# Hybrid decoder step: operand tiles at one residue modulo 256 bytes, states in the scratch buffers' tails

## The chip, the cores and the metric

The kernel runs on one core of one Trainium2 chip. The metric is the device time of one execution in microseconds. Three runs of the kernel before took 1388.89, 1389.11 and 1389.2 us; the median is 1389.11.

## The reference

One layer of a hybrid decoder trunk, for 256 prompt tokens and 8 sample tokens (264 columns in all), model width 2048, all in float32:

```python
xn = rms_norm(x, g_mix)
z = xn @ w_in                      # 2048 x 3584: pool | lru x | lru gelu gate | conformer a | b
y_pool = pool_mixer(u_pool, pool_buf, ...) @ w_pool_br          # 512 -> 2048
xc, new_lru_buf = causal_dwconv(lru_buf, u_lru, w_lru_conv, b_lru_conv)      # 4 taps
h, h_last = rg_lru(xc, lru_h, ...)                              # 8 block-diagonal gates, scan
y_lru = (h * gelu(u_gel)) @ w_lru_br                            # 1024 -> 2048
vc, new_conf = causal_dwconv(conf_buf, c_a * sigmoid(c_b), w_conf_conv, b_conf_conv)  # 31 taps
y_conf = silu(layer_norm(vc, g_conf, b_conf)) @ w_conf_br       # 512 -> 2048
g_a, g_b, g_c = split(sigmoid(xn @ w_gate + b_gate), 3)
x = x + (g_a * y_pool + g_b * y_lru + g_c * y_conf) @ w_out
hid = square(relu(rms_norm(x, g_mlp) @ w_up))                   # 2048 -> 8192
x = x + hid @ w_down                                            # 8192 -> 2048
y = rms_norm(x, g_final)
```

The prompt starts from empty states; the sample tokens come with states of the pool (15 rows), the LRU's convolution (3 rows), its hidden vector, and the conformer's convolution (30 rows). All states are returned, brought forward by one step.

## The kernel before

*Products.* Features lie on the 128 partitions and the 264 tokens along the free dimension. Every matmul has 128 x 128 weights and 264 moving columns. To keep float32's precision, both sides are split into a high part, rounded to the `float32r` type, and a low part, the rest; `mm3` adds three matmuls: high weights by high operand (line 204), high weights by low operand (205), low weights by high operand (206). Line 913 issues the same three for the first four chunks in another order, so that operands can be used as they arrive.

*The stream of weights.* All weights come in chunks of 1,024 columns (two K tiles by four column tiles of 128), so a dense chunk is 24 matmuls: for each of its two K tiles, four column tiles by three. `weight_plan` lists the chunks in the order of use: `w_in`, then gates with the branch products of pool, LRU and conformer between them, `w_out`, and four times a quarter of `w_up` and the matching quarter of `w_down`. `dma_pair` (SP's queue, lines 148 and 156) loads two chunks into `raw`, which has 6 slots; `split` (lines 187 on ACT and 188 on DVE) makes `whi` and `wlo`, with 4 slots each, three chunks ahead of PE.

*Moving operands.* Tiles are allocated one after another, so their places follow from the sizes and the order.

- `A` holds 32 operand tiles, 16 high and 16 low: first `xn`, then the merged branches, then the hidden layer of quarters 0 and 2. It is addressed through `operand`: `SHIFT` = 56 floats further in, with a pitch of `PITCH` = 320 floats.
- `xn2` (four tiles that reuse the four scratch buffers `B`, in `bpart`) holds the second normalised input, in the same way: 8 operands in each.
- `L` and `LH` (one buffer, tag "L") hold the LRU's operands, and `Q` (tag "Q") those of the pool and the conformer. They are plain arrays `[P, 16, N]`, so their pitch is N = 264 floats, 1,056 bytes. In quarters 1 and 3 of the hidden layer `LH` holds the high parts and `Q` the low ones (`hid`).

*The rest.* DVE, ACT and POOL do normalisation, convolutions, gates and scans in between. Their order is written by hand: `stage` and `run_bg` deal pieces of it out, a chunk at a time, when the program is built; each engine then works strictly in that order and waits on semaphores.

*States.* All sample states lie in one tile `st`, of 2,036 floats a partition: 1,824 come in with one DMA (line 952) right after the first weights, in chunk 2; all go out with one DMA (line 983) in chunk 140. `pool_evac` (line 673) and `ca_evac` (line 582) add the newest row of the pool and conformer states; `diff` (709, 710) and the conformer's `products` (605) read them. `vext`, the conformer's padded input, lies at the end of the first 2,112 floats of the fourth scratch buffer; the first 2,112 floats of each are used as eight tiles of 264 (`B`), and the last 448 are in use for `xn2` alone.

*The end.* After the last product, DVE, ACT and POOL normalise `X` and write it to `y`, in two halves, and SP and ACT send it out (lines 1002 to 1026).

Of the kernel before, what the change touches and what calls it, by code (L numbers as in the profile page):

```python
# [9 lines left out]
F32 = mybir.dt.float32  # L10
F32R = mybir.dt.float32r
# [4 lines left out]
P = 128  # L16
# [22 lines left out]

S_POOL, S_LC, S_CC, S_H = 0, 512, 768, 1760  # L40
S_IN = 1824
# [3 lines left out]
PITCH = 320  # L45
SHIFT = 56
HEAD = N + 512
# [42 lines left out]
def hybrid_step(ctx: ExitStack, tc: tile.TileContext, first, par_in, st_in, wall, y_out, st_out):  # L90
# [11 lines left out]
    wlo = cpool.tile([P, NHI, CH], F32R, name="wlo")  # L102
    a_all = cpool.tile([P, SHIFT + 31 * PITCH + N], F32R, name="A")
    b_all = [cpool.tile([P, SHIFT + 7 * PITCH + N], F32, name=f"tmp{i}", tag=f"B{i}") for i in range(4)]
    qtmp = cpool.tile([P, 16 * N], F32, name="qtmp", tag="Q")
    X = cpool.tile([P, KD, N], F32, name="X")
    B = [b[:, :8 * N].rearrange("p (a n) -> p a n", a=8) for b in b_all]
    L = cpool.tile([P, 16, N], F32R, name="L", tag="L")
    G = cpool.tile([P, 24, N], F32, name="G")
    par = cpool.tile([P, NPAR], F32, name="par")  # L110
    st = cpool.tile([P, S_OUT], F32, name="st")
    rstd = cpool.tile([P, N], F32, name="rstd")
    ones = cpool.tile([P, P], F32, name="ones")
# [9 lines left out]
    def operand(t, k):  # L123
        at = SHIFT + k * PITCH
        return t[:, at:at + N]

# [99 lines left out]
    def later(n, fn):  # L226
        delayed.append((now[0] + n, fn))
# [56 lines left out]
    def rms_close(pk):  # L284
        ps = ones_mm(pk)
        inverse_root(rstd, ps[:, :N], 1.0, G[:, 9, :])
        spend(dve=1.4, act=0.8)
# [57 lines left out]
    def x_sum():  # L345
        nc.vector.tensor_tensor(sq4[:, 0:2, :], sq4[:, 0:2, :], sq4[:, 2:4, :], op=ALU.add)
        nc.vector.tensor_tensor(sq4[:, 0, :], sq4[:, 0, :], sq4[:, 1, :], op=ALU.add)
        spend(dve=1.2)
        later(1, lambda: total_fold(L[:, 0, :], G[:, 10, :], sq4[:, 0, :]))

    def x_rms():
        rms_close(L[:, 0, :])
        later(1, lru_x_scale)
# [24 lines left out]

    st_lc = st[:, S_LC:S_LC + 256].rearrange("p (c b k) -> p c b k", c=8, b=8)
    st_cc = st[:, S_CC:S_CC + 992].rearrange("p (c b k) -> p c b k", c=4, b=8)  # L380
    st_po = st[:, S_POOL:S_POOL + 512].rearrange("p (c b k) -> p c b k", c=4, b=8)
    st_h = st[:, S_H:S_H + 64].rearrange("p (c b) -> p c b", c=8)
    XC = G[:, 0:8, :]
# [6 lines left out]
    def LH(s):  # L390
        if not l_at:
            l_at.append(cpool.tile([P, 16, N], F32R, name="LH", tag="L"))
        return l_at[0][:, s, :]

    def two(c):
        return slice(2 * c, 2 * c + 2)
# [41 lines left out]
    def lru_conv_sample():  # L438
        tmp = CT.rearrange("p c n -> p (c n)")[:, :256].rearrange("p (c b k) -> p c b k", c=8, b=8)
        xs = XC[:, :, TP:N]  # L440

        def products():
            wb = pv("w_lru_conv").rearrange("p (c k) -> p c k", c=8)[:, :, None, :].to_broadcast([P, 8, 8, 4])
            nc.gpsimd.tensor_tensor(tmp, st_lc, wb, op=ALU.mult)
            nc.gpsimd.tensor_copy(st[:, O_LC:O_LC + 24].rearrange("p (c k) -> p c k", c=8), el[:, :, TP:TP + 3])

        def sums():
            nc.vector.tensor_reduce(xs, tmp, op=ALU.add, axis=AX.X)
            nc.vector.tensor_tensor(xs, xs, pv("b_lru_conv")[:, :, None].to_broadcast([P, 8, 8]), op=ALU.add)

        stage("lru", "pool", 1.0, [products])
        stage("lru", "dve", 0.5, [sums])
# [6 lines left out]

    def lo_two(t, at=8):  # L460
        return lambda c: t[:, at + 2 * c:at + 2 * c + 2, :]

    def hi_two(t):
        return lambda c: t[:, 2 * c:2 * c + 2, :]

    def lru_gate_mm(ct, c, j):
        assert "xc" in done
        hi, lo = whi[:, c % NHI, :], wlo[:, c % NHI, :]
        out = []
        for t in range(2):  # L470
            s = slice((2 * j + t) * P, (2 * j + t + 1) * P)
            ps = acc()
            mm3(ps, hi[:, s], lo[:, s], L[:, ct, :], L[:, 8 + ct, :], True, True)
            out.append(ps)
        nc.scalar.activation(RA[:, ct, :], out[0][:, :N], AF.Sigmoid, bias=pv("b_lru_a", ct))
        nc.scalar.activation(TM[:, ct, :], out[1][:, :N], AF.Sigmoid, bias=pv("b_lru_x", ct))
        spend(act=1.0)
        if ct % 2:
            def times():
                nc.vector.tensor_tensor(XC[:, ct - 1:ct + 1, :], XC[:, ct - 1:ct + 1, :], TM[:, ct - 1:ct + 1, :],  # L480
                                        op=ALU.mult)
                spend(dve=0.71)

            later(1, times)

    def lru_tail():
# [3 lines left out]
        def scratch():  # L490
            S.append(cpool.tile([P, 16, N], F32, name="lscr", tag="L")[:, 0:8, :])

# [30 lines left out]
        def sample():  # L523
            hs = H[:, :, TP:N]
            nc.gpsimd.tensor_tensor(TM[:, :, TP:N], TM[:, :, TP:N], st_h, op=ALU.mult)
            nc.gpsimd.tensor_tensor(hs, hs, TM[:, :, TP:N], op=ALU.add)
            nc.gpsimd.tensor_copy(st_h, hs)
            nc.gpsimd.tensor_copy(st[:, O_H:O_H + 8], H[:, :, TP - 1])

# [50 lines left out]
    def ca_evac(ct, ps):  # L580
        nc.vector.tensor_tensor(vext[:, ct, 30:], ps[:, :TP], SG[:, ct, :TP], op=ALU.mult)
        nc.vector.tensor_tensor(st_cc[:, ct, :, 30], ps[:, TP:N], SG[:, ct, TP:], op=ALU.mult)
        spend(dve=0.5)

    def conf():
# [17 lines left out]
        def products():  # L603
            wb = pv("w_conf_conv").rearrange("p (c k) -> p c k", c=4)[:, :, None, :].to_broadcast([P, 4, 8, 31])
            nc.gpsimd.tensor_tensor(tmp, st_cc, wb, op=ALU.mult)
            nc.gpsimd.tensor_copy(st[:, O_CC:O_CC + 120].rearrange("p (c k) -> p c k", c=4), vext[:, :, TP:TP + 30])

# [63 lines left out]
    def pool_evac(gi, ps):  # L671
        nc.vector.tensor_tensor(pext[:, gi, 15:], ps[:, :TP], rstd[:, :TP], op=ALU.mult)
        nc.vector.tensor_tensor(st_po[:, gi, :, 15], ps[:, TP:N], rstd[:, TP:], op=ALU.mult)
        spend(dve=0.5)
# [6 lines left out]
    def Q(s):  # L681
        if not q_at:
            q_at.append(cpool.tile([P, 16, N], F32R, name="Q", tag="Q"))
        return q_at[0][:, s, :]

    def pooling():
# [9 lines left out]
        def rows():  # L696
            nc.gpsimd.tensor_copy(st[:, O_POOL:O_POOL + 60].rearrange("p (c k) -> p c k", c=4),
                                  pext[:, :, TP:TP + 15])

        def diff(gi):  # L700
            w = 2 << gi
            s = part(gi + 1, gi)[:, 0, 15:]
            d = DU[:, gi, :]
            u = pext[:, gi, 15:]
            nc.vector.scalar_tensor_tensor(d[:, 16:TP], s[:, 16:], 1.0 / w, u[:, 16:], op0=ALU.mult, op1=ALU.subtract)
            nc.vector.scalar_tensor_tensor(s[:, :16], pv("count"), 1.0 / w, s[:, :16], op0=ALU.max, op1=ALU.mult)
            nc.vector.tensor_tensor(d[:, :16], s[:, :16], u[:, :16], op=ALU.subtract)
            us = st_po[:, gi, :, 15]
            nc.vector.tensor_reduce(d[:, TP:N], st_po[:, gi, :, 16 - w:], op=ALU.add, axis=AX.X)
            nc.vector.scalar_tensor_tensor(d[:, TP:N], d[:, TP:N], 1.0 / w, us, op0=ALU.mult, op1=ALU.subtract)  # L710
# [21 lines left out]
    def bpart(k):  # L732
        if not M:
            M.extend(cpool.tile([P, SHIFT + 7 * PITCH + N], F32R, name=f"xn2{i}", tag=f"B{i}") for i in range(4))
        return operand(M[k // 8], k % 8), operand(M[2 + k // 8], k % 8)
# [149 lines left out]
    def after(gi):  # L885

        name, _, _, m = groups[gi]
        if name == "w_in":
            if m == 2:
                lru_conv(range(4, 8))  # L890
                lru_conv_sample()
                mark("lru", "conv")
                stage_split("lru", 4, hi_two(L), lo_two(L), lambda c: XC[:, 2 * c:2 * c + 2, :])
                mark("lru", "xc")
# [41 lines left out]
    for i, ch in enumerate(chunks):  # L936
# [13 lines left out]
        if i == 2:  # L950
            nc.sync.dma_start(par, par_in)
            nc.sync.dma_start(st[:, :S_IN], st_in)
        kind, gi, c, _ = ch
# [26 lines left out]
        if i == len(chunks) - 4:  # L980
            nc.scalar.preload_act_table_set(ROOT)
        if i == 140:
            nc.sync.dma_start(st_out, st)
        if 5 <= i < 9:
# [15 lines left out]
    for h in range(2):  # L1000
        for k, t in enumerate((20, 21 + (KD - 2) % 3, 11)):
            nc.tensor.matmul(ps[h][:, :H2], ones, G[:, t, half[h]], start=k == 0, stop=k == 2)  # L1002
    out = [cpool.tile([P, SHIFT + 7 * PITCH + N], F32, name=f"y{h}", tag=f"B{h}")[:, :KD * H2]
           .rearrange("p (k n) -> p k n", k=KD) for h in range(2)]
# [131 lines left out]
```

## Time and profile before

| | us |
|---|---|
| median of 3 runs (lowest to highest) | 1389.11 (1388.89 to 1389.2) |
| span of the profiled execution | 1387.7 |
| PE busy, in that span | 1377.4 |
| DVE busy | 836.2 |
| ACT busy | 722.1 |
| POOL busy | 93.5 |

The profiled execution is one of its own; its span runs from the first to the last instruction on the chip, and the median of the runs stands 1.4 us above it. Memory is read at 184 GB/s over the span (252.57 MB).

How to read the rows: a group's row gives the line, the engine, the operation, what it writes and reads, the number of instructions, then the total busy time and the mean duration of one in ns, and the idle time before them with what ended it. PE is the matmul itself, PEld the load of its weights, which overlaps. A row by tile gives the shortest, median and longest duration in ns, and the first and last start in us. A row by window gives the window, its length, busy time and instructions of PE, the granted clock (1.00 is full speed), the mean busy share of the 16 DMA engines, and GB/s. A row of the timeline gives the start and the duration in us. A row of a wait gives who waited for whom: the sum in us, how often, the longest. A row of DMA issues ends with the KB of one and the us from issue to landing.

### The profile page before, as it was taken

How to read it: one execution, taken by the hardware profiler on the slowest of the kernel's cores; microseconds unless marked ns; L12 is line 12 of the kernel's file. 1: busy time of each engine (PE TensorE's matmuls, PEld its weight loads, DVE VectorE, ACT ScalarE, POOL GpSimd, SP SyncE). 2: the span in 40 equal slices, each digit the busy share in tenths (PEclk: the TensorE clock that was granted, in tenths of full speed). 3: DMA queues.
4: the chain of work that ended last, by engine and by line, in shares of the span. 5: the costliest groups of instructions: out<-in, count | busy, mean ns of one | idle time of the engine just before them, and what ended most of it. 6: DMA issues, size and time to landing. Idle time of an engine off the chain costs nothing.

```text
span 1387.7 us, 26639 instructions
## 1 busy us (share of the span) xinstructions
PE 1377.4 (99%) x11421; PEld 1375.6 (99%) x11421; DVE 836.2 (60%) x1052; ACT 722.1 (52%) x1021; POOL 93.5 (7%) x122
## 2 busy tenths in 40 slices
PE   9999999999999999999999999999999999999997
PEld 9999999999999999999999999999999999999997
DVE  8785887776766658566555445554455544455544
ACT  7757576666664645455544334543344533354544
POOL 0220010110102013010000000000000000000012
PEclk9999999999999999999999999999999999999999
DMA  9555555555565554655555555555555555555551
GB/s 355 180 178 189 189 187 195 182 182 184 181 214 181 182 185 156 209 178 173 198 184 185 183 183 186 183 182 178 178 184 183 184 186 182 187 183 184 179 177 72
DMA packets 39670, 257.49 MB, mean 186 GB/s; under 512 B 4352, under 2 KB 5504, under 8 KB 10624
## 3 DMA queue, kind: packets, MB, share of 16 engines
q1 hardware_dynamic: 39120, 255.19, 53.9%
q8 instruction: 89, 1.46, 0.4%
q10 hardware_dynamic: 432, 0.61, 0.1%
q14 instruction: 29, 0.24, 0.0%
HBM read 252.57 MB, written 3.21 MB: 184 GB/s over the span
## 4 chain that ended last, share of the span: by engine, by line
PE 99%; DVE 0%; DVEq 0%; ACT 0%; issue 0%
PE acc L204 33%; PE acc L205 33%; PE acc L206 32%; PE acc L913 1%; PE acc L298 0%; DVE y L1025 0%; DVE acc L1016 0%; DVEq L1115 0%; DVE G L1015 0%; DVE acc L1014 0%; PE acc L1002 0%; PE acc L281 0%; ACT rstd L1009 0%; DVE G L844 0%; DVE X L843 0%
## 5 line engine op out<-in xcount | busy, mean ns | idle before, releaser
L188 DVE TENSOR_TENSOR wlo<-raw,whi 128x1024 fp32r<-128x1024 f32 (+1 forms) x478 | 584.6, 1225 | 526.7 <-ACT whi L187 526.4
L187 ACT CAST whi<-raw 128x1024 fp32r<-128x1024 f32 (+1 forms) x478 | 495.3, 1039 | 599.5 <-PE acc L205 549.2
L204 PE MATMUL acc<-A,whi 128*128 128x264 f32 x1952 | 551.3, 282 | 0.0
L205 PE MATMUL acc<-A,whi 128*128 128x264 f32 x1952 | 551.2, 282 | 0.0
L206 PE MATMUL acc<-A,wlo 128*128 128x264 f32 x1952 | 548.6, 281 | 0.0
L206 PEld LDWEIGHTS acc<-A,wlo 128*128 128x128 f32 x1952 | 366.2, 188 | 0.0
L205 PEld LDWEIGHTS acc<-A,whi 128*128 128x128 f32 x1952 | 365.9, 187 | 0.0
L204 PEld LDWEIGHTS acc<-A,whi 128*128 128x128 f32 x1952 | 365.7, 187 | 0.0
L204 PE MATMUL acc<-xn,whi 128*128 128x264 f32 x1024 | 290.0, 283 | 0.0
L205 PE MATMUL acc<-xn,whi 128*128 128x264 f32 x1024 | 288.9, 282 | 0.0
L206 PE MATMUL acc<-xn,wlo 128*128 128x264 f32 x1024 | 287.2, 281 | 0.0
L206 PEld LDWEIGHTS acc<-xn,wlo 128*128 128x128 f32 x1024 | 192.2, 188 | 0.0
L205 PEld LDWEIGHTS acc<-xn,whi 128*128 128x128 f32 x1024 | 192.0, 188 | 0.0
L204 PEld LDWEIGHTS acc<-xn,whi 128*128 128x128 f32 x1024 | 191.7, 187 | 0.0
L205 PE MATMUL acc<-Q,whi 128*128 128x264 f32 x644 | 182.9, 284 | 0.0
L204 PE MATMUL acc<-LH,whi 128*128 128x264 f32 x640 | 182.3, 285 | 0.0
L206 PE MATMUL acc<-LH,wlo 128*128 128x264 f32 x640 | 181.9, 284 | 0.0
L205 PEld LDWEIGHTS acc<-Q,whi 128*128 128x128 f32 x644 | 121.7, 189 | 0.0
L206 PEld LDWEIGHTS acc<-LH,wlo 128*128 128x128 f32 x640 | 120.7, 189 | 0.0
L204 PEld LDWEIGHTS acc<-LH,whi 128*128 128x128 f32 x640 | 120.6, 188 | 0.0
L814 POOL TENSOR_TENSOR G<-G 128x264 f32<-128x264 f32 x28 | 25.7, 919 | 799.8 <-ACT G L812 798.9
L595 ACT ACTIVATE G<-tmp,par 128x256 f32<-128x256 f32 x120 | 54.3, 500 | 1.4 <-DVE G L609 0.7
(194 smaller groups left out, 792.7 us busy)
## 6 DMA issues: line engine op xcount, KB each, us to landing
raw<-wall_dram SPq DMA_DIRECT2D x226, 1024.0 KB, 4.9
raw<-wall_dram SPq DMA_DIRECT2D x12, 512.0 KB, 7.7
raw<-first_dram SPq DMA_DIRECT2D x6, 512.0 KB, 7.8
X<-first_dram SPq DMA_DIRECT2D x6, 264.0 KB, 7.3
raw<-wall_dram SPq DMA_DIRECT2D x5, 256.0 KB, 3.0
tmp<-first_dram SPq DMA_DIRECT2D x3, 388.0 KB, 4.8
so_dram<-st SPq DMA_DIRECT2D x1, 1018.0 KB, 9.4
st<-st_dram SPq DMA_DIRECT2D x1, 912.0 KB, 9.3
```

Of the source, the lines that this page charges most:

```text
L187: nc.scalar.copy(h[:, s], r[:, s])
L188: nc.vector.tensor_tensor(lo[:, s], r[:, s], f(h[:, s]), op=ALU.subtract)
L204: nc.tensor.matmul(ps[:, :N], whi_t, xh, start=first, stop=False)
L205: nc.tensor.matmul(ps[:, :N], whi_t, xl, start=False, stop=False)
L206: nc.tensor.matmul(ps[:, :N], wlo_t, xh, start=False, stop=last)
L595: nc.scalar.activation(dst[:, ct, :TP], vext[:, ct, k:k + TP], AF.Copy, scale=par[:, w:w + 1])
L814: nc.gpsimd.tensor_tensor(sq2, sq2, t, op=ALU.add)
L913: nc.tensor.matmul(pss[m][:, :N], w[:, i % NHI, s], x, start=i == kt == k == 0, stop=False)
```

## The change

`SHIFT` goes. `par` and `rstd` are allocated ahead of `A` instead of near the end, so that `A` and the tiles after it start at byte 96 modulo 256 by themselves. `L`, `LH` and `Q` get the pitch of 320 floats and are read through `operand` (one tile) and the new `operands` (several); splits and the LRU's square roots, which wrote two adjoining tiles of 264, now write two tiles 320 floats apart. `qtmp` and `L` thereby grow from 4,224 to 5,120 floats.

Room for that comes out of `st`, which shrinks to 532 floats: the pool and conformer states (376 floats a partition for each of the four groups) now lie in the four scratch buffers, from float 2,112 on (`tails`). They come in with four DMAs in chunks 13 to 16, after the weight pair that is issued in an even chunk, and go out with four in chunks 136 to 139. The conformer's `products` on POOL becomes four instructions, one for each group. On the host, the layout of the state arrays follows. The order of PE's instructions and what they wait for stay as they were.

```diff
-S_POOL, S_LC, S_CC, S_H = 0, 512, 768, 1760
+TAIL = 376
+S_SMALL = 4 * TAIL
+S_LC, S_H = S_SMALL, S_SMALL + 256
...
-SHIFT = 56
...
-    a_all = cpool.tile([P, SHIFT + 31 * PITCH + N], F32R, name="A")
-    b_all = [cpool.tile([P, SHIFT + 7 * PITCH + N], F32, name=f"tmp{i}", tag=f"B{i}") for i in range(4)]
-    qtmp = cpool.tile([P, 16 * N], F32, name="qtmp", tag="Q")
+    par = cpool.tile([P, NPAR], F32, name="par")
+    rstd = cpool.tile([P, N], F32, name="rstd")
+    a_all = cpool.tile([P, 32 * PITCH], F32R, name="A")
+    b_all = [cpool.tile([P, 8 * PITCH], F32, name=f"tmp{i}", tag=f"B{i}") for i in range(4)]
+    qtmp = cpool.tile([P, 16 * PITCH], F32, name="qtmp", tag="Q")
+    L = cpool.tile([P, 16 * PITCH], F32R, name="L", tag="L")
     X = cpool.tile([P, KD, N], F32, name="X")
...
-    L = cpool.tile([P, 16, N], F32R, name="L", tag="L")
     G = cpool.tile([P, 24, N], F32, name="G")
-    par = cpool.tile([P, NPAR], F32, name="par")
-    st = cpool.tile([P, S_OUT], F32, name="st")
-    rstd = cpool.tile([P, N], F32, name="rstd")
+    st = cpool.tile([P, S_OUT - S_SMALL], F32, name="st")
...
     def operand(t, k):
-        at = SHIFT + k * PITCH
-        return t[:, at:at + N]
+        return t[:, k * PITCH:k * PITCH + N]
+
+    def operands(t, k, n=2):
+        return t[:, k * PITCH:(k + n) * PITCH].rearrange("p (k c) -> p k c", k=n)[:, :, :N]
...
+    tails = [b[:, 8 * N:8 * N + TAIL] for b in b_all]
+    st_po = [t[:, :128].rearrange("p (b k) -> p b k", b=8) for t in tails]
+    st_cc = [t[:, 128:].rearrange("p (b k) -> p b k", b=8) for t in tails]
+
+    def state_move(i, move):
+        move(tails[i], slice(i * TAIL, (i + 1) * TAIL))
...
-            l_at.append(cpool.tile([P, 16, N], F32R, name="LH", tag="L"))
-        return l_at[0][:, s, :]
+            l_at.append(cpool.tile([P, 16 * PITCH], F32R, name="LH", tag="L"))
+        return operands(l_at[0], s.start) if isinstance(s, slice) else operand(l_at[0], s)
...
-            mm3(ps, hi[:, s], lo[:, s], L[:, ct, :], L[:, 8 + ct, :], True, True)
+            mm3(ps, hi[:, s], lo[:, s], operand(L, ct), operand(L, 8 + ct), True, True)
...
-            nc.gpsimd.tensor_tensor(tmp, st_cc, wb, op=ALU.mult)
+            for ct in g4:
+                nc.gpsimd.tensor_tensor(tmp[:, ct], st_cc[ct], wb[:, ct], op=ALU.mult)
...
-            q_at.append(cpool.tile([P, 16, N], F32R, name="Q", tag="Q"))
-        return q_at[0][:, s, :]
+            q_at.append(cpool.tile([P, 16 * PITCH], F32R, name="Q", tag="Q"))
+        return operands(q_at[0], s.start) if isinstance(s, slice) else operand(q_at[0], s)
...
         if i == 2:
             nc.sync.dma_start(par, par_in)
-            nc.sync.dma_start(st[:, :S_IN], st_in)
+            nc.sync.dma_start(small(S_SMALL, S_IN - S_SMALL), st_in[:, S_SMALL:])
+        if 13 <= i < 17:
+            state_move(i - 13, lambda t, s: nc.sync.dma_start(t, st_in[:, s]))
...
+        if 136 <= i < 140:
+            state_move(i - 136, lambda t, s: nc.sync.dma_start(st_out[:, s], t))
         if i == 140:
-            nc.sync.dma_start(st_out, st)
+            nc.sync.dma_start(st_out[:, S_SMALL:], st)
```

More of the change, by code (lines that the diff above doesn't have):

```diff
@@ L348, in x_sum @@
         spend(dve=1.2)
-        later(1, lambda: total_fold(L[:, 0, :], G[:, 10, :], sq4[:, 0, :]))
+        later(1, lambda: total_fold(operand(L, 0), G[:, 10, :], sq4[:, 0, :]))
     def x_rms():
-        rms_close(L[:, 0, :])
+        rms_close(operand(L, 0))
         later(1, lru_x_scale)
@@ L376, in softplus, with small @@
         eng.tensor_scalar(sp[:, 8:16], t2, -8.0, 0.0, op0=ALU.mult, op1=ALU.add)
[L379 to L382, printed above, removed]
+    def small(at, n):
+        return st[:, at - S_SMALL:at - S_SMALL + n]
+    tails = [b[:, 8 * N:8 * N + TAIL] for b in b_all]
+    st_lc = small(S_LC, 256).rearrange("p (c b k) -> p c b k", c=8, b=8)
+    st_po = [t[:, :128].rearrange("p (b k) -> p b k", b=8) for t in tails]
+    st_cc = [t[:, 128:].rearrange("p (b k) -> p b k", b=8) for t in tails]
+    st_h = small(S_H, 64).rearrange("p (c b) -> p c b", c=8)
+    def state_move(i, move):
+        move(tails[i], slice(i * TAIL, (i + 1) * TAIL))
     XC = G[:, 0:8, :]
@@ L444, in products @@
             nc.gpsimd.tensor_tensor(tmp, st_lc, wb, op=ALU.mult)
-            nc.gpsimd.tensor_copy(st[:, O_LC:O_LC + 24].rearrange("p (c k) -> p c k", c=8), el[:, :, TP:TP + 3])
+            nc.gpsimd.tensor_copy(small(O_LC, 24).rearrange("p (c k) -> p c k", c=8), el[:, :, TP:TP + 3])
         def sums():
@@ L458, in stage_split @@
                                for i in range(n)], gap)
[L460 to L464, printed above, removed]
     def lru_gate_mm(ct, c, j):
@@ L490, in scratch @@
         def scratch():
-            S.append(cpool.tile([P, 16, N], F32, name="lscr", tag="L")[:, 0:8, :])
+            S.append(operands(cpool.tile([P, 16 * PITCH], F32, name="lscr", tag="L"), 0, 8))
         def tanh(ct):
@@ L527, in sample @@
             nc.gpsimd.tensor_copy(st_h, hs)
-            nc.gpsimd.tensor_copy(st[:, O_H:O_H + 8], H[:, :, TP - 1])
+            nc.gpsimd.tensor_copy(small(O_H, 8), H[:, :, TP - 1])
         c4 = range(4)
@@ L581, in ca_evac @@
         nc.vector.tensor_tensor(vext[:, ct, 30:], ps[:, :TP], SG[:, ct, :TP], op=ALU.mult)
-        nc.vector.tensor_tensor(st_cc[:, ct, :, 30], ps[:, TP:N], SG[:, ct, TP:], op=ALU.mult)
+        nc.vector.tensor_tensor(st_cc[ct][:, :, 30], ps[:, TP:N], SG[:, ct, TP:], op=ALU.mult)
         spend(dve=0.5)
@@ L604, in products @@
             wb = pv("w_conf_conv").rearrange("p (c k) -> p c k", c=4)[:, :, None, :].to_broadcast([P, 4, 8, 31])
-            nc.gpsimd.tensor_tensor(tmp, st_cc, wb, op=ALU.mult)
-            nc.gpsimd.tensor_copy(st[:, O_CC:O_CC + 120].rearrange("p (c k) -> p c k", c=4), vext[:, :, TP:TP + 30])
+            for ct in g4:
+                nc.gpsimd.tensor_tensor(tmp[:, ct], st_cc[ct], wb[:, ct], op=ALU.mult)
+            nc.gpsimd.tensor_copy(small(O_CC, 120).rearrange("p (c k) -> p c k", c=4), vext[:, :, TP:TP + 30])
         def sums():
@@ L672, in pool_evac @@
         nc.vector.tensor_tensor(pext[:, gi, 15:], ps[:, :TP], rstd[:, :TP], op=ALU.mult)
-        nc.vector.tensor_tensor(st_po[:, gi, :, 15], ps[:, TP:N], rstd[:, TP:], op=ALU.mult)
+        nc.vector.tensor_tensor(st_po[gi][:, :, 15], ps[:, TP:N], rstd[:, TP:], op=ALU.mult)
         spend(dve=0.5)
@@ L696, in rows @@
         def rows():
-            nc.gpsimd.tensor_copy(st[:, O_POOL:O_POOL + 60].rearrange("p (c k) -> p c k", c=4),
+            nc.gpsimd.tensor_copy(small(O_POOL, 60).rearrange("p (c k) -> p c k", c=4),
                                   pext[:, :, TP:TP + 15])
@@ L707, in diff @@
             nc.vector.tensor_tensor(d[:, :16], s[:, :16], u[:, :16], op=ALU.subtract)
-            us = st_po[:, gi, :, 15]
-            nc.vector.tensor_reduce(d[:, TP:N], st_po[:, gi, :, 16 - w:], op=ALU.add, axis=AX.X)
+            us = st_po[gi][:, :, 15]
+            nc.vector.tensor_reduce(d[:, TP:N], st_po[gi][:, :, 16 - w:], op=ALU.add, axis=AX.X)
             nc.vector.scalar_tensor_tensor(d[:, TP:N], d[:, TP:N], 1.0 / w, us, op0=ALU.mult, op1=ALU.subtract)
@@ L733, in bpart @@
         if not M:
-            M.extend(cpool.tile([P, SHIFT + 7 * PITCH + N], F32R, name=f"xn2{i}", tag=f"B{i}") for i in range(4))
+            M.extend(cpool.tile([P, 8 * PITCH], F32R, name=f"xn2{i}", tag=f"B{i}") for i in range(4))
         return operand(M[k // 8], k % 8), operand(M[2 + k // 8], k % 8)
@@ L892, in after @@
                 mark("lru", "conv")
-                stage_split("lru", 4, hi_two(L), lo_two(L), lambda c: XC[:, 2 * c:2 * c + 2, :])
+                stage_split("lru", 4, lambda c: operands(L, 2 * c), lambda c: operands(L, 8 + 2 * c),
+                            lambda c: XC[:, two(c), :])
                 mark("lru", "xc")
@@ L1002, in hybrid_step @@
             nc.tensor.matmul(ps[h][:, :H2], ones, G[:, t, half[h]], start=k == 0, stop=k == 2)
-    out = [cpool.tile([P, SHIFT + 7 * PITCH + N], F32, name=f"y{h}", tag=f"B{h}")[:, :KD * H2]
+    out = [cpool.tile([P, 8 * PITCH], F32, name=f"y{h}", tag=f"B{h}")[:, :KD * H2]
            .rearrange("p (k n) -> p k n", k=KD) for h in range(2)]
@@ L1092 @@
     par = np.ascontiguousarray(np.concatenate(par, 1))
-    st = np.ascontiguousarray(np.concatenate([
-        _rows(a["state_pool"][0], 1), _rows(a["state_lru_conv"][0], 1), _rows(a["state_conf_conv"][0], 1),
-        _rows(a["state_lru_h"][0][:, None, :], 0)], 1))
+    big = np.concatenate([_rows(a["state_pool"][0], 1).reshape(P, 4, -1),
+                          _rows(a["state_conf_conv"][0], 1).reshape(P, 4, -1)], 2).reshape(P, -1)
+    st = np.ascontiguousarray(np.concatenate([big, _rows(a["state_lru_conv"][0], 1),
+                                              _rows(a["state_lru_h"][0][:, None, :], 0)], 1))
     wall = _stream({n: a[n][0] for n in ("w_in", "w_pool_grp", "w_pool_br", "w_lru_a", "w_lru_x", "w_lru_br",
@@ L1122, with rows_s @@
     ys = np.ascontiguousarray(y[TP:])[:, None]
-    def rows_s(at, c, k):
-        v = so[:, at:at + c * TS * k].reshape(P, c, TS, k)[..., 1:]
+    tails = so[:, :S_SMALL].reshape(P, 4, TAIL)
+    def rows_s(v, c, k):
+        v = v.reshape(P, c, TS, k)[..., 1:]
         return np.ascontiguousarray(v.transpose(2, 3, 1, 0).reshape(1, TS, k - 1, c * P))
@@ L1134 @@
     return (yp, ys, rows_p(O_POOL, 4, 15), rows_p(O_LC, 8, 3), h_p, rows_p(O_CC, 4, 30),
-            rows_s(S_POOL, 4, 16), rows_s(S_LC, 8, 4), h_s, rows_s(S_CC, 4, 31))
+            rows_s(tails[:, :, :128], 4, 16), rows_s(so[:, S_LC:S_LC + 256], 8, 4), h_s, rows_s(tails[:, :, 128:], 4, 31))
```

## The prediction

> **What bounds the kernel now.** I read the page first: which engine is busy, at what clock, and what the chain that ended last is made of.
>
> ```profile
> span 1387.7 us, 26639 instructions
> PE 1377.4 (99%) x11421; PEld 1375.6 (99%) x11421; DVE 836.2 (60%) x1052; ACT 722.1 (52%) x1021; POOL 93.5 (7%) x122
> PEclk9999999999999999999999999999999999999999
> PE 99%; DVE 0%; DVEq 0%; ACT 0%; issue 0%
> ```
>
> PE is busy for 1377.4 of 1387.7 us at the full granted clock, and the chain is PE for 99%. Next the waits, longest first, to see whether PE ever waits for an operand.
>
> ```profile
> ACT whi L187 <- PE acc L205: 549.2, 350, 3.7
> ...
> PE acc L298 <- PEq L1109: 0.8, 1, 0.8
> ```
>
> The casts of the streamed weights wait for PE to give their buffers back, 549.2 us in all; of PE there is only the 0.8 us at its start. So the time is the number of matmuls times their spacing, plus a head and a tail. The mean duration in the rows (about 282 ns) is not the spacing: matmuls overlap. For the spacing I took, by tile, the first and last start in two `w_down` quarters, first the one that reads `A`, then the one that reads `LH` and `Q`.
>
> ```profile
> L204 PE MATMUL acc<-A,whi x256: 285/285/285, 728.6 to 820.4; 128*128 128x264 f32 x128
> L206 PE MATMUL acc<-A,wlo x256: 279/279/279, 728.8 to 820.6; 128*128 128x264 f32 x128
> L204 PE MATMUL acc<-LH,whi x256: 278/285/294, 912.9 to 1006.0; 128*128 128x264 f32 x128
> L206 PE MATMUL acc<-LH,wlo x256: 278/283/297, 913.1 to 1006.3; 128*128 128x264 f32 x128
> ```
>
> Same 768 matmuls, same shapes: 728.6 to 820.6 against 912.9 to 1006.3, 92.0 against 93.4 us. The durations are also constant for `A` (285/285/285) and scattered for `LH` (278 to 297). To have it to 0.01 us, I cut the windows from the first matmul of a stage to the first after it: four times the branch products of pool and LRU together, those of the conformer, and three `w_down` quarters, the first of which is the `A` one. The counts include the two or three matmuls still running at the left edge.
>
> ```profile
> 243.16:260.63 17.47, 17.47 (x146) 1.00 0.55 183
> 283.67:301.16 17.49, 17.49 (x146) 1.00 0.53 183
> 347.24:364.73 17.49, 17.49 (x147) 1.00 0.53 183
> 410.81:428.29 17.48, 17.48 (x146) 1.00 0.62 213
> 520.72:544.14 23.42, 23.42 (x194) 1.00 0.44 149
> 728.58:820.74 92.16, 92.16 (x770) 1.00 0.54 184
> 912.90:1006.38 93.48, 93.48 (x770) 1.00 0.53 181
> 1282.86:1376.35 93.49, 93.49 (x771) 1.00 0.41 139
> ```
>
> The `A` quarter is 92.16 us for 768, **120.0 ns** each. The `LH`/`Q` ones are 93.48, **121.7 ns**, at the same clock and with no more DMA traffic (shares 0.53 and 0.41 against 0.54). What differs is where the moving operand lies. Tiles lie in the order of their allocation. In the built program `raw` starts at byte 1,152 of a partition and all tiles up to `G` are multiples of 256 bytes long, so each starts at byte 128 modulo 256. `A(k)` lies `SHIFT` (56 floats, 224 bytes) further in, at 96, and its pitch of 1,280 is 5 x 256: every `A` and `xn2` operand is at 96 modulo 256. `L`, `LH` and `Q` have a pitch of 1,056 = 4 x 256 + 32, so tile k starts at 128 + 32k modulo 256: only k = 7 and 15 lie at 96, k = 4 and 12 at 0.
>
> Does the time follow that within one tile? The timeline of the second column group of the `LH`/`Q` quarter has twelve matmuls in a row on each k; these are the first rows of k = 4, 5, 6, 7 and 8, residues 0, 32, 64, 96 and 128:
>
> ```profile
> 942.09 0.29 PE L204 MATMUL acc<-LH,whi 128*128 128x264 f32 x1
> ...
> 943.57 0.29 PE L204 MATMUL acc<-LH,whi 128*128 128x264 f32 x1
> ...
> 945.04 0.28 PE L204 MATMUL acc<-LH,whi 128*128 128x264 f32 x1
> ...
> 946.50 0.29 PE L204 MATMUL acc<-LH,whi 128*128 128x264 f32 x1
> ...
> 947.95 0.28 PE L204 MATMUL acc<-LH,whi 128*128 128x264 f32 x1
> ```
>
> Steps of 1.48, 1.47, 1.46 and 1.45 us: 123.3, 122.5, 121.7 and 120.8 ns a matmul. The run at 96 is the fastest of the four.
>
> **The change part by part.**
>
> *Operands.* `L`, `LH` and `Q` get the pitch of 1,280, and every operand tile starts at 96 modulo 256 (`par` and `rstd` now stand ahead of `A`: 58,496 + 1,200, up to the next 32, + 1,056 = 60,768 = 237 x 256 + 96). `A` and `xn2` move by exactly 2,048 bytes, so their 120.0 ns should stay. `LH` and `Q` come to lie 20,480 bytes apart, as `A`'s high and low halves do; weights, PSUM and PE's order are untouched. I take 120.0 ns for all. Branch products: 17.47 + 17.49 + 17.49 + 17.48 = 69.93 us for 4 x 144 matmuls, against 69.12 at 120.0: 0.81 us. Conformer: 23.42 against 192 x 0.120 = 23.04: 0.38. The two quarters: 93.48 and 93.49 against 92.16: 1.32 + 1.33. The LRU gate blocks and the pool groups have no windows of their own:
>
> ```profile
> L204 PE MATMUL acc<-L,whi 128*128 128x264 f32 x16 | 4.5, 283 | 0.0
> ```
>
> 16 of each of three products, and 4 x 3 for the pool groups, 60 matmuls at the mean excess of the others, 3.84 us / 2,304 = 1.67 ns: 0.10. Together **3.94 us**. The other end of the bound is the `LH` row at 96 itself, 120.8 ns; I take 120.0 because the 1.45 us includes the step from a neighbour at another residue, which the `A` rows, with no such neighbour, don't have.
>
> *States.* One 912 KB load becomes 160 KB at the old place and four pieces of 188 KB (1,504 bytes a partition) in SP's queue, after the weight pairs of chunks 20, 22 (two pieces) and 24. The rows that bound it:
>
> ```profile
> raw<-wall_dram SPq DMA_DIRECT2D x226, 1024.0 KB, 4.9
> ...
> st<-st_dram SPq DMA_DIRECT2D x1, 912.0 KB, 9.3
> ...
> y_dram<-y SPq DMA_DIRECT2D x2, 198.0 KB, 2.0
> ...
> par<-par_dram SPq DMA_DIRECT2D x1, 150.0 KB, 7.6
> 42.36 15.66 SPq L148 DMA_DIRECT2D raw<-wall_dram  x3
> L673 DVE TENSOR_TENSOR st<-acc,rstd x4: 161/164/164, 74.3 to 75.6; 128x8 f32<-128x8 f32 x4
> ```
>
> The three pairs are issued from 42.36 to 58.02. A piece lands in between 2.0 (198 KB, DMA otherwise quiet) and 9.3 us (the whole old load in the crowded head); I take 4.9, that of a weight pair beside the same stream. The last lands by 58.4 + 9.3 = 67.7 at the latest. The four `L673` results, which now go into the pieces and so wait for them, come from 74.3 on: 6.6 us of cover, value 0. Behind them on DVE stand the weight splits, and PE waits for those, so from there on a late piece would cost first their lead and then PE time. The weight loads queued behind the pieces have cover too: chunk 20's load is issued at 42.36 and cast here:
>
> ```profile
> 54.78 1.04 ACT L187 CAST whi<-raw 128x1024 fp32r<-128x1024 f32 x1
> 4.56 12.47 PE acc L913 x96
> ```
>
> PE ends its first four chunks at 17.03 and takes 24 x 0.120 = 2.88 us for each later one, so it needs chunk 20 at about 63.1. Less cast and subtraction, 1.04 and about 1.2, the load may land until 60.8, 18.4 us after issue; it takes 4.9, which leaves 13.5. The states' way out, five DMAs of the old 1,018 KB, goes out beside the gates from about 400 us on and nobody reads it: 0.
>
> *POOL and the splits.* The conformer products are four instructions instead of one.
>
> ```profile
> 173.86 3.13 POOL L605 TENSOR_TENSOR G<-st,par 128x992 f32<-128x992 f32 x1 [35.95 <-DVE st L582]
> 192.27 1.18 DVE L609 TENSOR_REDUCE G<-G 128x32 f32<-128x992 f32 x1
> L444 POOL TENSOR_TENSOR G<-st,par x1: 644/644/644, 83.0 to 83.0; 128x256 f32<-128x256 f32 x1
> L428 DVE TENSOR_TENSOR G<-G,tmp x6: 1218/1219/2548, 58.7 to 87.4; 128x1024 f32<-128x1024 f32 x6
> L339 DVE TENSOR_TENSOR G<-G x3: 1250/1253/1253, 29.2 to 33.8; 128x1056 f32<-128x1056 f32 x3
> ```
>
> Four like `L444` are 2.6 us, four times the whole row 12.5; the sum that needs them starts at 192.27, 15.3 us after `L605` ends, so even the upper end, 9.4 us more, is covered. Splits and roots that wrote 528 contiguous elements now write 2 x 264 with a gap: `L428`, in the code four pieces of 256, has 1.19 ns an element, `L339`, in one, 1.19 too. Cost 0.
>
> *Head and tail.* The first 96 matmuls (12.47 us) wait for loads that the change leaves alone. `X`, `G` and `y` start 32 bytes lower modulo 256:
>
> ```profile
> L849 DVE TENSOR_TENSOR X<-X,acc x63: 420/423/430, 751.0 to 1375.1; 128x264 f32<-128x264 f32 x63
> ```
>
> `L849` goes through all eight residues of `X` and spreads by 10 ns of 423, 2.4%; on the about 11.3 us of the tail that is at most 0.3 either way. I take 0.
>
> Sum: 1387.7 - 3.9 = 1383.8 us of span. The median of the runs, 1389.11, is 1.4 above that profile's span, so **1385.2 us**.
>
> **The rivals.** *Half the gain.* `LH` and `Q` settle at the 120.8 ns of their own rows at 96: 2,364 x (121.67 - 120.83) = 2.0 us, 1387.1. For it: these are their own rows. Against it: the jump between residues is in them.
>
> *No change: the residue is not the cause*, and the scatter belongs to these two tiles, whatever their place: 1389.1. The four steps from 1.48 to 1.45 inside one tile speak against it. [...]
>
> *Slower: the pieces hold up the weights.* If each of the three pieces ahead of chunk 24's load took the old load's 9.3 us and they went one after another, it would come 27.9 us later; 13.5 are covered, 14.4 fall on PE, less the 3.9 gained: 1399.6. It decides from 17.4 us of delay on. For it: 1,504-byte rows in the middle of the stream. Against it: the traffic there is 0.53 to 0.56 of the engines' time, 188 KB is less than a fifth of a weight pair, which lands in 4.9, and the 912 KB of before at the crowded head did no harm.
>
> **How the numbers follow.** Forecast 0.83, half the gain 0.07, no change 0.05, slower 0.05. The range, 1384.6 to 1386.6, is the forecast with 0.3 for head and tail and the 0.31 us between the lowest and highest run below, and above with 0.8 more, for a part of the matmuls staying over 120.0 ns. A change under 0.2% (2.8 us) can't be told from none, so half the gain counts as the same: faster 0.84, same 0.11, slower 0.05.
>
> **What would show it.** Right: the `LH`/`Q` quarters take 92.16 us and their durations are as constant as `A`'s, the first of them starts at about 911.6 (1.3 earlier) and the last matmul of the stream ends 3.9 earlier. Half: 92.8 us. Wrong on the cause: 93.5 us again. Wrong on the cover: a row of PE waiting for `wlo` between 45 and 80 us, or of DVE `L673`'s successor waiting for a state DMA.

## The result and the profile after

The changed kernel took 1385.35 us (median of 7 runs, 1384.94 to 1385.68); the kernel before, beside it, 1389.2 (7 runs, 1388.89 to 1390.07). The ratio is 0.9971, with a 95% interval of 0.9961 to 0.9982: 0.3% faster, small but clear of the spread of the runs. 1385.2 was predicted.

The page of the changed kernel, the lines on the span, the engines and the chain:

```profile
span 1383.8 us, 26656 instructions
PE 1373.5 (99%) x11421; PEld 1371.8 (99%) x11421; DVE 835.4 (60%) x1052; ACT 721.5 (52%) x1021; POOL 94.4 (7%) x125
PE 99%; DVE 0%; DVEq 0%; ACT 0%; issue 0%
```

The span is 3.9 us shorter and PE is busy for 3.9 us less with the same 11,421 matmuls; the rest of the page hardly moved. Where they went is seen in the view by windows, cut as before from the first matmul of a stage to the first after it: four times the branch products of pool and LRU, those of the conformer, the `A` quarter of `w_down`, and the two `LH`/`Q` quarters.

```profile
243.12:260.40 17.28, 17.28 (x146) 1.00 0.53 187
283.44:300.72 17.28, 17.28 (x146) 1.00 0.53 184
346.80:364.08 17.28, 17.28 (x146) 1.00 0.54 184
410.16:427.44 17.28, 17.28 (x146) 1.00 0.55 187
519.86:542.90 23.04, 23.04 (x194) 1.00 0.43 153
727.35:819.51 92.16, 92.16 (x770) 1.00 0.54 184
911.67:1003.83 92.16, 92.16 (x770) 1.00 0.54 183
1280.31:1372.47 92.16, 92.16 (x770) 1.00 0.41 141
```

Each of these stages now has 120.0 ns a matmul. The branch products gave 17.47 + 17.49 + 17.49 + 17.48 - 4 x 17.28 = 0.81 us, the conformer's 0.38, the quarters 1.32 and 1.33. From the first LRU gate block to the first of these windows, by the starts in the traces, it is 139.68 us in place of 139.78: 0.10 for the gate blocks and the pool groups. Together that is the 3.94 of the sum. The view by tile, for `LH` in the first of the two quarters, shows that the scatter of the durations (278 to 297 before) is gone too:

```profile
L207 PE MATMUL acc<-LH,whi x256: 282/283/283, 911.7 to 1003.5; 128*128 128x264 f32 x128
L209 PE MATMUL acc<-LH,wlo x256: 285/285/285, 911.9 to 1003.7; 128*128 128x264 f32 x128
```

The covers held. The first rows below are the state pieces (the view of line 961 and the time to landing of its DMAs), then the DVE instruction that needs them, then the POOL products and the sum behind them (timeline).

```profile
L961 SPq DMA_DIRECT2D tmp<-st_dram x4: 425/432/434, 42.8 to 58.1; - x4
...
DMA to landing us min/median/max: 4.9/5.2/5.9
...
L679 DVE TENSOR_TENSOR tmp<-acc,rstd x4: 164/166/167, 74.4 to 75.6; 128x8 f32<-128x8 f32 x4
...
172.62 4.03 POOL L611 TENSOR_TENSOR G<-tmp,par 128x248 f32<-128x248 f32 x4 [34.68 <-issue]
...
192.26 1.18 DVE L615 TENSOR_REDUCE G<-G 128x32 f32<-128x992 f32 x1
```

The last piece landed by 58.1 + 5.9 = 64.0, ten us before it is used, and the four products ended at 176.7, 15.6 before the sum. PE waited for no weights and no states: its only waits are 0.8 us at its start and 0.3 us for the last normalisation in the tail, both as before.

```profile
PE acc L301 <- PEq L1121: 0.8, 1, 0.8
...
PE acc L1013 <- DVE G L850: 0.3, 1, 0.3
```

### The profile page after: what moved, and what is told of

Read it like the earlier page. It is cut to its first block, busy times and chain, and to the rows that moved or that the text cites. A ratio compares the mean times of both kernels' runs of the same rounds, so it can differ in the third digit from the quotient of the medians.

```text
span 1383.8 us, 26656 instructions
## 1 busy us (share of the span) xinstructions
PE 1373.5 (99%) x11421; PEld 1371.8 (99%) x11421; DVE 835.4 (60%) x1052; ACT 721.5 (52%) x1021; POOL 94.4 (7%) x125
## 4 chain that ended last, share of the span: by engine, by line
PE 99%; DVE 0%; DVEq 0%; ACT 0%; issue 0%
PE acc L209 33%; PE acc L208 33%; PE acc L207 32%; PE acc L920 1%; PE acc L301 0%; DVE y L1036 0%; DVE acc L1027 0%; DVEq L1127 0%; DVE G L1026 0%; DVE acc L1025 0%; PE acc L1013 0%; PE acc L284 0%; ACT rstd L1020 0%; DVE G L850 0%; DVE X L849 0%
## 5 line engine op out<-in xcount | busy, mean ns | idle before, releaser
L209 PE MATMUL acc<-xn,wlo 128*128 128x264 f32 x1024 | 291.7, 285 | 0.0
```

Source lines behind the costliest of these rows:

```text
L209: nc.tensor.matmul(ps[:, :N], wlo_t, xh, start=False, stop=last)
```

## The experiments

Two questions stayed open. Was it the placement that gave the 3.9 us, or did the moved states and tiles give or take something beside it? And is it the operand's own place that sets the spacing, or the step between places, or the place relative to something else? Each edit is to the changed kernel. Residue means the start of an operand modulo 256 bytes; the weights start at 128 unless said otherwise. "Inner" spacings are means over the starts in the trace, with the first and the last of the twelve steps on one operand left out. e3 to e7 were run once each.

### e1: the old pitch back

`L`, `LH` and `Q` are read through functions of their own, `lq` for one tile and `lqs` for several. The first tile starts 8 floats further in, at residue 128 as before:

```diff
+    def lqs(t, k, n=2):
+        at = 8 + k * N
+        return t[:, at:at + n * N].rearrange("p (k c) -> p k c", k=n)[:, :, :N]
```

> The changed kernel, with L, LH and Q back at a pitch of 264 floats and at the residues they had before (128 + 32k modulo 256); the states stay in the tails and everything else as changed. Theory (the start of the moving operand modulo 256 sets the spacing; states, POOL and the strided splits cost nothing): the LH/Q quarters take 93.5 us again, the conformer's products 23.4, and the time is that of the kernel before, 1389.2. Rival (the moved states, the four POOL products or the new places of X and G gain or cost something that the operands hide): a time that differs from 1389.2 by that something, by more than 0.5 us, with A's quarter off 92.16.

Measured: 1389.05 us (10 runs), ratio to the kernel before 0.9998 (0.9989 to 1.0008). The windows for the conformer's products, the `A` quarter and the two others:

```profile
520.30:543.69 23.39, 23.39 (x194) 1.00 0.43 151
728.14:820.30 92.16, 92.16 (x770) 1.00 0.53 183
912.46:1005.94 93.48, 93.48 (x770) 1.00 0.53 182
1282.42:1375.90 93.48, 93.48 (x770) 1.00 0.40 139
```

With the residues of before, the stages take their old 23.4 and 93.48 us, states in the tails or not. So the placement of `L`, `LH` and `Q` is the whole gain, and the rest of the change costs nothing that can be measured: the kernel before had 1389.3 us beside this run, 0.25 more.

### e2: one pitch, another residue

`lq` and `lqs` again, with the changed kernel's pitch and 40 floats further in:

```diff
+    def lq(t, k):
+        return t[:, 40 + k * PITCH:40 + k * PITCH + N]
```

> The changed kernel with every L, LH and Q operand 160 bytes further in, so all of them start at residue 0 modulo 256, with the pitch of 1280 bytes kept. Theory (the residue itself sets the spacing): 123.6 ns a matmul as k = 4 and 12 had before, 94.9 us a quarter, 2,364 x 3.6 ns = 8.5 us more than the changed kernel: 1393.9. Rival (what cost was the step from one residue to another, or a pitch that is no multiple of 256): 120.0 ns, 92.16 us a quarter, 1385.4.

Measured: 1393.44 us (7 runs), ratio to the kernel before 1.0029 (1.0018 to 1.004). The conformer's products, the `A` quarter, the first `LH`/`Q` quarter:

```profile
521.40:545.06 23.66, 23.66 (x194) 1.00 0.43 148
729.52:821.68 92.16, 92.16 (x770) 1.00 0.54 184
913.84:1008.56 94.72, 94.72 (x770) 1.00 0.52 179
```

123.3 ns a matmul with a pitch of 1,280 bytes and no step between residues: the even pitch alone is worth nothing, and a badly chosen residue is 4.1 us worse than the uneven one of before. The rival falls. The place matters.

### e3: a scan of residues

```diff
+    def stepped(t, k, step, of):
+        at = k * PITCH + (step * (of % 16)) % 60
+        return t[:, at:at + N]
...
-        return operand(a_all, k)
+        return stepped(a_all, k, 4, k)
...
-        return operand(M[k // 8], k % 8), operand(M[2 + k // 8], k % 8)
+        return stepped(M[k // 8], k % 8, 1, k), stepped(M[2 + k // 8], k % 8, 1, k)
```

> The changed kernel with A(k) starting 16 bytes further in for each k, so its operands go through the residues 96, 112, ... to 240 and 0 to 64 modulo 256 (14 steps, then k = 15 at 96 again), and xn2 operand k starting 4 bytes further in for each k (96 to 156). L, LH and Q stay at 96. Theory: the spacing within a run of twelve matmuls on one k depends on the residue, as in LH and Q before: at 0 about 123.6 ns, 32 and 64 about 122, 128 and 160 about 121.4, 192 about 120.7, 224 about 122, at 96 120.0; what residues between multiples of 32 give is not known. The time then is some 1.5 ns x 5,952 matmuls of A = 9 us over the changed kernel, and some more for xn2. Rival (steps between residues): only the first matmul of a run is longer, by about 5 ns, the rest have 120.0; under 3 us more.

Measured: 1398.85 us (one run). Inner spacings of `A`: 122.3 ns at 0, 119.9 at 16, 120.6 at 48, 122.7 at 64, 120.1 at 96 and 144, 121.3 to 122.1 from 160 to 240. In steps of 4 bytes, `xn2` has 120.0 at 96 and 120, but 124.9 at 100 and 125.7 at 116. The first rows of neighbouring operands in one column group of `w_up` show it, at 96, 100 and 104, then at 116, 120 and 124:

```profile
663.84 0.28 PE L211 MATMUL acc<-xn,whi 128*128 128x264 f32 x1
...
665.28 0.28 PE L211 MATMUL acc<-xn,whi 128*128 128x264 f32 x1
...
666.77 0.29 PE L211 MATMUL acc<-xn,whi 128*128 128x264 f32 x1
...
671.18 0.28 PE L211 MATMUL acc<-xn,whi 128*128 128x264 f32 x1
...
672.69 0.29 PE L211 MATMUL acc<-xn,whi 128*128 128x264 f32 x1
...
674.13 0.28 PE L211 MATMUL acc<-xn,whi 128*128 128x264 f32 x1
```

Twelve matmuls took 1.44 us at 96 and 120, 1.49 at 100 and 1.51 at 116. So it isn't a matter of coarse alignment: 16, 48 or 144 serve as well as 96, or nearly, and 4 bytes can cost 5 ns.

### e4: the weights moved

```diff
+    par = cpool.tile([P, NPAR], F32, name="par")
+    rstd = cpool.tile([P, N], F32, name="rstd")
     whi = cpool.tile([P, NHI, CH], F32R, name="whi")
     wlo = cpool.tile([P, NHI, CH], F32R, name="wlo")
-    par = cpool.tile([P, NPAR], F32, name="par")
-    rstd = cpool.tile([P, N], F32, name="rstd")
```

> The changed kernel with par and rstd allocated ahead of whi and wlo instead of behind them: the weights start at residue 96 modulo 256 instead of 128, and all operands stay where they are. Theory (the moving operand's own place decides): 120.0 ns everywhere, 1385.4. Rival (the place relative to the weights decides, best when the operand lies 32 bytes below them modulo 256): an operand at the weights' own residue had 121.3 ns (128) before, so some 1.4 ns x 11,300 matmuls = 16 us more, about 1401.

Measured: 1387.76 us (one run), between the two expectations. Windows of 100 us, with every operand at 96, show why:

```profile
100.00:200.00 100.00, 100.00 (x836) 1.00 0.57 192
450.00:550.00 100.00, 100.00 (x826) 1.00 0.51 174
728.00:828.00 100.00, 100.00 (x835) 1.00 0.54 188
```

836 matmuls in 100 us are 120 ns each, 826 are 121.3 (the counts include two or three still running at the left edge). Matmuls of the same kind on the same places have two spacings, for hundreds of us at a time. Neither theory had that.

### e5: the scan with the weights moved

The edits of e3 and e4 together.

> The residue scan of e3 (A in steps of 16 bytes, xn2 in steps of 4) with the weights at residue 96 as in e4. Theory, place of the operand alone: the spacing by residue as in e3 (A: 16, 96 and 144 at 120, 0 at 122.3, 64 at 122.7, 224 at 122.1 ns). Rival, distance between operand and weights: the same profile 32 bytes lower, so 240, 64 and 112 at 120.0, and 224 (122.3), 32 (122.7) and 192 (122.1) the slow ones, 96 at 121.1 as 128 had.

Measured: 1399.99 us (one run). Inner spacings of `A` in ns:

| residue | e5 (weights at 96) | e3 at the same residue | e3 32 bytes higher |
|---|---|---|---|
| 240 | 119.96 | 121.70 | 119.93 |
| 64 | 119.99 | 122.66 | 120.12 |
| 112 | 120.01 | 121.33 | 120.09 |
| 16 | 120.53 | 119.93 | 120.61 |
| 32 | 122.78 | 121.76 | 122.66 |
| 224 | 122.80 | 122.13 | 122.28 |

The table has six of the fourteen residues that can be compared. Over all fourteen, e5 differs from e3 32 bytes higher by 0.17 ns in the mean, and from e3 at the same residue by 0.94. So the pattern moved with the weights, by their 32 bytes. In the timeline it is seen from the first rows of neighbouring operands in one column group: in e3 those at 240, 0, 16 and 32,

```profile
793.75 0.29 PE L211 MATMUL acc<-A,whi 128*128 128x264 f32 x1
...
795.21 0.29 PE L211 MATMUL acc<-A,whi 128*128 128x264 f32 x1
...
796.70 0.29 PE L211 MATMUL acc<-A,whi 128*128 128x264 f32 x1
...
798.14 0.28 PE L211 MATMUL acc<-A,whi 128*128 128x264 f32 x1
```

and in e5 those at 208, 224, 240 and 0:

```profile
792.10 0.29 PE L211 MATMUL acc<-A,whi 128*128 128x264 f32 x1
...
793.56 0.29 PE L211 MATMUL acc<-A,whi 128*128 128x264 f32 x1
...
795.04 0.29 PE L211 MATMUL acc<-A,whi 128*128 128x264 f32 x1
...
796.49 0.28 PE L211 MATMUL acc<-A,whi 128*128 128x264 f32 x1
```

Twelve matmuls at 0 took 1.49 us in e3, those at 224 took 1.48 in e5, and the next operand was quick again (1.44, 1.45). The theory that the operand's own residue decides falls here, and the distance to the weights takes its place. It does not fit everywhere: with steps of 4 bytes, e5's 100 has 125.9 ns where e3's 132 has 122.5, and over the eight residues that can be compared the mean difference is 0.8 ns, against 1.3 at the same residue. The two largest misses, at 96 and 100, are the first operands behind the jump back from 156; whether what ran before matters was not tested.

### e6: high and low parts apart

Only `Q` goes through e2's `lq` and `lqs`:

```diff
-        return operands(q_at[0], s.start) if isinstance(s, slice) else operand(q_at[0], s)
+        return lqs(q_at[0], s.start) if isinstance(s, slice) else lq(q_at[0], s)
```

> The changed kernel with Q alone at residue 0, L and LH at 96. In the two LH/Q quarters of w_down two matmuls of three then read at 96 and one at 0. Theory, each matmul pays for its own operand: 120.0 + 3.33 / 3 = 121.1 ns, 93.0 us a quarter; the products on Q alone (pool, conformer) at 123.3. Rival, the pair matters (a high and a low part at different residues): another value, 120.0 or over 122.

Measured: 1389.76 us (one run); the first `LH`/`Q` quarter:

```profile
912.41:1006.27 93.86, 93.86 (x771) 1.00 0.53 181
```

93.86 / 768 = 122.2 ns, where one third of e2's excess would give 121.1: one bad operand of three costs two thirds of what three cost. The theory falls and the rival's "over 122" holds: the excess doesn't add up matmul by matmul. How it comes about was not followed further.

### e7: another good residue

e2's edit with 44 floats in place of 40.

> The changed kernel with L, LH and Q all at residue 16 (176 bytes further in). Theory, as e3's scan has it: 16 is as good as 96, 120.0 ns, 92.16 us a quarter, 1385.4. Rival, all operand tiles have to share one residue (96): more than 120.0 ns in the LH/Q stages, 121 or more, 1387.8 or more.

Measured: 1385.7 us (one run), the first `LH`/`Q` quarter 92.15 us, 120.0 ns. `A` and `xn2` stay at 96, so the tiles don't have to share a residue: with the weights at 128, 16 is as good as 96.

### e8: e4 once more

> e4's kernel again, weights at residue 96, for the two spacings that its one trace had in turns (120.0 and 121.4 ns over hundreds of us with the same operands and weights). Theory, two stable rhythms between operand reads and weight loads, between which small things decide: the two spacings again, in other stretches of time, and runs that spread by several us between 1385 and 1401. Rival, they belong to the stages: the same stretches, and runs within 0.5 us of e4's 1387.8.

Measured: 1393.23 us median, with 10 runs from 1385.68 to 1399.96, eight of them between 1392.46 and 1393.81. The profiled one, in two windows of 100 us and the `A` quarter:

```profile
100.00:200.00 100.00, 100.00 (x826) 1.00 0.55 187
300.00:400.00 100.00, 100.00 (x826) 1.00 0.54 183
734.18:826.34 92.16, 92.16 (x771) 1.00 0.53 183
```

Here the window from 100 to 200 us, quick in e4, is slow. With operand and weights at the same residue, 96, PE has two rhythms and holds either for long: the theory of two rhythms stands, though no row shows that they lie between operand reads and weight loads. In the starts, the quick one repeats after four matmuls (steps of 122, 122, 120 and 116 ns, for one) and the slow one after five (126, 124, 116, 120 and 121).

The traces also show where the rhythm can change. Four single matmuls of line 284, which sum over the partitions for the normalisations with `ones_r` as weights, stand between the others. These are the second and the fourth in e4, with the windows on both sides of the second, and the fourth in e8's profiled run:

```profile
438.77 0.28 PE L284 MATMUL acc<-Q,ones_r 128*128 128x264 f32 x1
654.50 0.28 PE L284 MATMUL acc<-LH,ones_r 128*128 128x264 f32 x1
...
338.70:438.70 100.00, 100.00 (x836) 1.00 0.57 190
438.90:538.90 100.00, 100.00 (x827) 1.00 0.52 179
...
659.18 0.28 PE L284 MATMUL acc<-LH,ones_r 128*128 128x264 f32 x1
```

In e4 the rhythm goes to quick at the first of the four (42.65 us), to slow at the second, stays slow at the third and goes to quick at the fourth (654.50). In e8's profiled run it is slow through the first three and quick from the fourth (659.18). No change falls anywhere else. So the rival was half right: the places of a change belong to the program, but not which rhythm follows, and what decides that is open. Of the other nine runs there is no trace, but the times fit: some 5,270 matmuls ahead of the fourth at 1.34 ns more make 1385.35 + 7.1 = 1392.4, about where eight of the ten runs lie; quick throughout would be 1385.4 (1385.68 was measured), and slow throughout, some 11,300 matmuls, 1400.5 (1399.96).

### e9: both 32 bytes lower

```diff
     def operand(t, k):
-        return t[:, k * PITCH:k * PITCH + N]
+        return t[:, 56 + k * PITCH:56 + k * PITCH + N]
```

with the same in `operands`, and e4's order of tiles. 56 floats are 224 bytes, so modulo 256 the operands start 32 bytes lower, at 64; e4's order puts the weights at 96.

> The changed kernel with the weights at residue 96 (as in e4 and e8) and all operands, A, xn2, L, LH and Q, at 64, so that the distance of 32 bytes between them is that of the changed kernel and both lie 32 bytes lower modulo 256. Theory, formed after e5 (the distance between operand and weights modulo 256 sets the spacing): 120.0 ns everywhere, 92.16 us a quarter, 1385.4, with runs within 0.5 us of each other. Rival (the operand's own residue, with the weights' place a small thing beside it): 64 had 122.7 ns in e3 and 122.8 in LH/Q before, 2.7 ns x 11,295 matmuls = 30 us more, 1416.

Measured: 1385.12 us (7 runs, 1384.8 to 1385.61), ratio to the kernel before 0.997 (0.9959 to 0.9981). The `A` and the first `LH`/`Q` quarter:

```profile
727.34:819.50 92.16, 92.16 (x770) 1.00 0.53 183
911.66:1003.82 92.16, 92.16 (x770) 1.00 0.53 183
```

64 was among the slowest residues with the weights at 128 (122.7 ns in e3, on the same chip), and is without any excess with the weights at 96. The rival is off by 30 us.

### e10: the best spot of the scan

e9's edit with 7 floats in place of 56, and the changed kernel's order of tiles.

> The changed kernel with all operands at residue 124 (28 bytes further in), weights at 128 as before. In e3's scan 124 had 119.83 ns in the inner matmuls of a run, under 120. Theory (120.0 is a floor that the place can't lower; the 119.83 are the recovery after a slow neighbour): 120.0 ns, 1385.4. Rival (a better place exists): 119.83 ns x 11,295 matmuls = 1.9 us less than the changed kernel, 1383.5.

Measured: 1385.39 us (8 runs), ratio to the kernel before 0.9971 (0.996 to 0.9982), the first `LH`/`Q` quarter 92.16 us. The 119.83 ns came of leaving out the first step: in e3's starts that step takes 121 or 122 ns at 124, the second 118 or 119 and the rest 120, which is 120.0 over all twelve. No place that was tried takes a whole stage under 120.0.

## Why the prediction was right

*PE bounds the kernel, and its spacing is what to look at.* Right, though the prediction left out PE's 0.3 us of waiting in the tail, which did not change. The mean durations of the groups would not have shown it: `LH` with high weights went from 285 to 282 ns there, and in the page of the changed kernel `A`'s three lines, all at 120.0, differ by as much (280, 283, 283).

*120.0 ns for all of L, LH and Q.* Right, to 0.01 us in each of the eight windows. The higher end, 120.8 from the row at 96 itself, was wrong for the reason given, and by rounding: e1 has those neighbours again, and there the twelve steps at 96 take 1.445 us, 120.4 ns each, and the inner ones 120.17.

*The residue as the cause.* Right that the place sets the spacing (e1, e2), and wrong in what it is measured from. The prediction put it as the start of the moving operand modulo 256, from rows in which the weights always start at 128. The period of 256 is in the trace of the kernel before: in the `LH`/`Q` quarter from 912.90 us, tiles k and k + 8, 8,448 = 33 x 256 bytes apart, have the same inner spacing to 0.03 ns (123.57 and 123.60 at 0, 120.15 and 120.17 at 96), and tiles four apart, at 0 and 128, don't (123.57 and 121.57). e5 and e9 show, for a shift of the weights by 32 bytes, that it is the distance between the two; in the changed kernel the operands start 32 bytes below the weights. That the number didn't suffer is luck in so far as the change leaves the weights where they are: a version that had moved them by the way, as e4 does, would have been predicted at 1385.2 too and takes 1385.7 to 1400.0.

*States, POOL and strided splits at nothing.* Right: 4.9 us was taken for the landing of a piece, 4.9 to 5.9 measured, well inside the cover; the POOL products took 4.03 us, between the 2.6 and 12.5 of the bound. e1 shows that together they cost nothing that can be measured.

*Head and tail at nothing.* Right: the stages account for 3.94 us, the last of their windows ends 3.88 earlier (1372.47 against 1376.35), and the span is 3.9 shorter.

*The rivals.* Half the gain and no change fell with the windows. Nor is it enough that the starts are multiples of 32 bytes: those of e1, e2 and the changed kernel all are, and they give 1389.05, 1393.44 and 1385.35. Slower, by late weights, fell with the landings and with PE's waits.

Why the distance matters was not shown. That operand reads and weight loads get in each other's way is a guess. It fits e4, e5, e8 and e9, since moving the weights alone changes the spacing of unmoved operands (e4 and e8 have 121.3 ns over long stretches where the changed kernel has 120.0); but no row shows a stall by itself. A rival would be that the writing of the weights by ACT and DVE gets in the way, and the trace of e2 speaks against it: in its two `LH`/`Q` quarters the twelve matmuls on one operand take 123.33 ns each where ACT, DVE and POOL are idle all the while (three cases), and 123.34 where ACT and DVE together spend 70% of that time or more on writing weights (61 cases).

## What to carry to other kernels

What follows was measured for one kind of matmul, 264 columns of float32 with new weights for each. Where PE is the bound, compare the starts of equal matmuls between stages. Here one had 120.0 ns and another 121.7 at the same clock, with 120.15 to 123.6 from tile to tile; what differed were the places of operand and weights, and the excess was had back by a pitch that keeps their distance the same modulo 256 bytes (92.16 us a quarter in place of 93.48). Choose that distance by measuring (a scan with a different offset for each tile costs one run), and move weights and operands together (e9: 1384.8 to 1385.61 us) or not at all: with the weights alone moved, e8 took 1385.68 to 1399.96. Take more than one run before believing a place: one of the ten runs of e8, at a poor place, took no longer than the changed kernel at its slowest.

## What was not expected of the hardware

- Moving the weights by 32 bytes, with all operands in place, gave runs from 1385.68 to 1399.96 us of the same program: two rhythms, of 120.0 and 121.3 ns a matmul, each held for hundreds of us, with every change in the two traces at one of four matmuls that use other weights (e4, e8).
- 4 bytes are enough to matter: 120.0 ns at 96, 124.9 at 100, 125.7 at 116 and 120.0 at 120 (e3, weights at 128).
- No placement that was tried took a whole quarter under 120.0 ns a matmul: e7, e9, e10 and the changed kernel, with operands 112, 32, 4 and 32 bytes below the weights modulo 256, have 92.15, 92.16, 92.16 and 92.16 us for its 768.
